# Low parts of the streamed weight blocks: a negated rounding on ScalarE and an accumulating GpSimd DMA instead of a VectorE subtraction

## The chip, the cores and the metric

The program runs on one NeuronCore of a Trainium2 chip. The metric is the device time of one execution in microseconds (us), and the time before is the median of three executions. Engines are named as in the profile: PE is TensorE's matmul stream and PEld its weight loads, DVE is VectorE, ACT is ScalarE, POOL is GpSimd, SP is SyncE, which in this kernel issues every DMA.

## The reference, cut to what matters

One inference step of a two-layer encoder trunk over 656 tokens (16 meta tokens, 512 prompt tokens, 8 streams of 16 new tokens), all in float32. Per layer:

```
h    = rmsnorm(x, g_mix);  proj = h @ w_in                 # 1024 -> 3072 columns
qa, ka, va, glu, zf, ic, qc, gc = split(proj)
oa   = differential attention (4 heads, relative-position bias, chunk mask)
ob   = swish(layernorm(causal depthwise conv of GLU, width 31))
oc   = gated linear recurrence (4 heads, 64 x 64 state)
x    = x + concat(oa, ob, oc) @ w_out                      # 1024 -> 1024
h2   = rmsnorm(x, g_ffn);  gate, val = split(h2 @ w_up)    # 1024 -> 2 x 2816
x    = x + (gelu(conv3(gate)) * val) @ w_down              # 2816 -> 1024
```

The outputs are the normalised x and the new keys, values and states. The weight products are wanted with nearly float32 accuracy, which is why both operands of each are split into two parts.

## The kernel before, in words

**Layout and products.** Channels lie on the 128 partitions, the 656 token columns on the free axis, in two halves of 328. Weights come from HBM in blocks of 128 x 128; a *block column* is the column of such blocks that makes 128 output channels. `w_load` (L327 to L331) gets a block column with one DMA of SP into a tile `raw`, of which the pool has NR = 3 buffers. `w_split` (L336 to L351) turns it into units of up to four row blocks (three where there are six): ACT rounds `raw` to the type fp32r in L347, which gives `whi`, and DVE makes `wlo = raw - whi` in L348. Both have NW = 4 buffers. The activations are split in the same way (`split`, L314). `mm3` (L356 to L361) then issues three matmuls for each row block, in the order hi times `whi`, lo times `whi`, hi times `wlo`, and adds them up in PSUM. So PE first needs a unit's `wlo` at its third matmul.

**Units kept apart.** With `own=True` the two parts go to buffers of the large pool `slots` (`ghi`, `glo`); this is used where a unit must be ready long ahead, at the start of a layer's projection and of the feed-forward, and in the last stage of the program. The feed-forward's gates and values are made by Strassen's method in `combos` (L938): POOL adds and subtracts weight halves (`wcb`, L944), and ACT and DVE split the results at L950 and L951, in the same four `whi` and `wlo` buffers.

**Stages of a layer.**

- Input projection: 24 block columns of eight row blocks, the first three together as a group. Between them stand the generators of attention, convolution and recurrence (`advance`), so DVE, ACT and POOL have much other work here.
- Output projection, first part (`d_oa`): 8 block columns of six row blocks, then the second part (`d_ob`): 8 of two row blocks, each followed by the residual add (`add_x`, L404), a square (L395, summed on POOL at L400) and the split of x (L322, L323).
- Feed-forward: pairs of gate and value block columns (G, V in the string FFN), and between them the down projection in parts (D0, D1, D2 of six row blocks, 8 block columns each; D3 of four). `add_x` adds each product to x. D3 of layer 0 also squares and splits x for the next layer; D3 of the last layer is the program's last stage, with `own` units.

**What sets the order.** The program is written in one order; a scheduler then sorts the instructions of each engine's queue by its own estimate, allots pool buffers and sets the waits. Every engine works its queue strictly in order. A conversion at L347 waits for its `raw` to land and for PE to have finished with the unit that held its `whi` buffer; with four buffers that is the unit four places before. A load waits until the last reader of its `raw` buffer is done. At the kernel's very start `start["on"]` keeps a few instructions in the written order (`seq`).

The lines the prediction speaks of:

```python
            seq(A.copy(hi[:, :n], raw[:, a:a + n]))
            seq(V.tensor_tensor(out=lo[:, :n], in0=raw[:, a:a + n], in1=hi[:, :n].bitcast(F32), op=ALU.subtract))
```

```python
        for j, (ww, r) in enumerate(((whi, hi), (whi, lo), (wlo, hi))):
            PE.matmul(ps[:, :b - a], lhsT=ww[:, n], rhs=r[:, a:b], start=first and j == 0, stop=last and j == 2)
```

Of the kernel before, what the change touches and what calls it, by code (L numbers as in the profile page):

```python
# [9 lines left out]
F32 = mybir.dt.float32  # L10
# [3 lines left out]
ALU = mybir.AluOpType  # L14
# [7 lines left out]
T = 656  # L22
# [22 lines left out]
# columns in two parts: all; behind 12 meta tokens; behind all meta tokens  # L45
# [9 lines left out]
# columns of the packed small operands  # L55
# [36 lines left out]
def pack(x):  # L92
    """layouts only: channels to rows, weights in blocks of 128 x 128"""
# [6 lines left out]
    small = dict(cst)  # L100
# [34 lines left out]
def unpack(r):  # L135
    """layouts only: back to the shapes of the reference"""
# [18 lines left out]
def trunk_kernel(ctx: ExitStack, tc: tile.TileContext, i: dict, o: dict, depth: int = 2):  # L155
# [51 lines left out]
    # gains that go with norm_r, which gives -2 / rms  # L207
# [21 lines left out]
    def setup():  # L229
# [35 lines left out]
        # relative-position bias times 8 (scores are scaled by 1/8 together with it)  # L265
# [25 lines left out]
    def norm_r(ones, srcs, nm, cc=CA):  # L291
        """-2 (ones^T-sum of srcs + eps) ** -0.5 on all partitions: table value and one Newton step."""
# [16 lines left out]
    def seq(ins):  # L309
        """in the order of the program at the kernel's start, where all inputs are on their way"""  # L310
        if start["on"]:
            tc.keep_in_program_order(ins)
            start[ins.ins.engine] = ins.ins
# [22 lines left out]
    def w_split(raw, kt, a=0, own=False):  # L336
        """hi and lo parts of row blocks a..kt: [(hi, lo, place in unit)] by k"""
        half = 4 if kt in (4, 8) else 3
        units = []
        while a < kt:  # L340
# [7 lines left out]
            seq(V.tensor_tensor(out=lo[:, :n], in0=raw[:, a:a + n], in1=hi[:, :n].bitcast(F32), op=ALU.subtract))  # L348
# [20 lines left out]
    def gemm(units, ks, rhs, nm, cc=CA, P=PD):  # L369
        """two psum[128, columns] = w^T rhs, float32 operands as hi + lo parts"""  # L370
        return [gemm1(units, ks, rhs, f"{c}_{nm}", cc[c], P) for c in range(2)]

    def gemm_group(unit_lists, ks, rhs, nm, cc=CA):
        """three products side by side, in the order in which the row blocks of rhs come"""
# [16 lines left out]
    def sq_add(m, ab=(0, T)):  # L391
        """accumulate x_m ** 2"""
# [20 lines left out]
    def tok_major(src, nm):  # L413
        """[128 tokens, 4, 128] of tokens 0..511, then [:, 512:640] samples; second tile: tokens 512..527."""
# [14 lines left out]
    def attention(l, h, got, mix):  # L429
# [32 lines left out]
        # prompt queries, tiles of 128 behind the meta tokens  # L462
# [59 lines left out]
        # running streams; the meta queries as a ninth stream without past keys  # L522
# [116 lines left out]
    def conv(l, t, got, accs):  # L639
# [11 lines left out]
        # last 30 inputs of each stream  # L651
# [629 lines left out]
```

## Time and profile before

| | |
|---|---|
| three executions, median (lowest, highest) | 1781.49 us (1781.0, 1783.29) |
| profiled execution, first to last instruction (its span) | 1784.5 us |
| mean granted TensorE clock | 0.968 |
| PE busy | 1650.5 us, 92% |
| PEld busy | 1550.3 us, 87% |
| DVE busy | 1327.3 us, 74% |
| ACT busy | 820.6 us, 46% |
| POOL busy | 596.2 us, 33% |
| bytes moved by DMA | 151.19 MB, 85 GB/s on average |

For the profiled execution the page gives its span, 1784.5 us, and no other time of its own. That is 3.0 us (0.17%) above the median of the three executions and 1.2 us above the slowest of them. A busy share is a mean over stages with different limits, so the sections below go by stage. Matmuls are pipelined: one record lasts 0.31 us, but in a dense stretch one starts every 0.15 us.

### The profile page before, as it was taken

The page shows a single profiled execution, that of the slowest core. Times are in us where ns is not written, and L with a number is a line of the kernel's source. Part 1 is how long each engine was busy: PE and PEld are TensorE (multiplying, and loading weights), DVE is VectorE, ACT ScalarE, POOL GpSimd, SP SyncE. Part 2 cuts the span into 40 slices and gives each one's busy share as a digit, 9 for nine tenths or more (in the row PEclk, how much of TensorE's full clock was granted, in tenths as well). Part 3 has the DMA queues.
Part 4 walks back from the last instruction along what each step waited for, and adds up shares of the span by engine and source line. Part 5 has one row for each costly group of instructions (what it writes and reads, how often), then busy time and mean ns, then how long its engine had stood idle before and what let it go on. Part 6 is the DMA issues. An engine that isn't in the chain of part 4 may idle for free.

```text
span 1784.5 us, 28714 instructions
## 1 busy us (share of the span) xinstructions
PE 1650.5 (92%) x10760; PEld 1550.3 (87%) x10760; DVE 1327.3 (74%) x2492; ACT 820.6 (46%) x1605; POOL 596.2 (33%) x620
## 2 busy tenths in 40 slices
PE   7769899999899999999999989899998999999897
PEld 6759687898889989988999978788988998999896
DVE  6159998759995884788556799866898668568855
ACT  5156364745442342444336545566535334343524
POOL 2012222004661551764021132300266256156503
PEclk9989999999999999999999999999999999999999
DMA  5223211234124222222332211213412422222132
GB/s 183 43 77 92 74 63 55 73 123 141 38 66 148 71 72 71 71 83 73 123 117 71 78 64 66 73 53 113 174 36 69 135 72 69 86 71 83 58 90 71
DMA packets 62270, 151.19 MB, mean 85 GB/s; under 512 B 11284, under 2 KB 16916, under 8 KB 62132
## 3 DMA queue, kind: packets, MB, share of 16 engines
q1 hardware_dynamic: 62132, 149.36, 25.8%
q8 instruction: 85, 1.39, 0.3%
q14 instruction: 53, 0.43, 0.1%
HBM read 129.80 MB, written 19.54 MB: 84 GB/s over the span
## 4 chain that ended last, share of the span: by engine, by line
PE 56%; DVE 23%; POOL 6%; DMA 5%; issue 5%; ACT 3%; DVEq 0%; SPq 0%; POOLq 0%; ACTq 0%
PE d_dn L361 16%; PE d_i L361 11%; PE d_v L361 6%; PE d_oa L361 5%; PE d_g L361 4%; DMA raw<-in_w_in 3%; POOL wcb L944 3%; DVE wlo L951 3%; DMA raw<-in_w_up 2%; PE e_i L361 2%; POOL gv L1210 2%; DVE fh L1025 2%; DVE ga L1047 2%; DVE cva L676 2%; PE sc L478 1%
## 5 line engine op out<-in xcount | busy, mean ns | idle before, releaser
L347 ACT CAST whi<-raw 128x384 fp32r<-128x384 f32 (+2 forms) x243 | 132.1, 547 | 330.7 <-PE d_dn L361 107.7
L361 PE MATMUL d_v<-fh,whi 128*128 128x328 f32 (+1 forms) x1120 | 261.2, 321 | 11.7 <-DVE gp L1173 6.2
L361 PE MATMUL d_g<-fh,whi 128*128 128x328 f32 (+1 forms) x1008 | 235.4, 321 | 11.9 <-ACT us_g L984 10.9
L361 PE MATMUL d_i<-hi_h,whi 128*128 128x328 f32 x672 | 219.1, 326 | 22.8 <-ACT whi L347 21.9
L348 DVE TENSOR_TENSOR wlo<-raw,whi 128x384 fp32r<-128x384 f32 (+2 forms) x243 | 155.3, 644 | 91.9 <-ACT whi L347 83.9
L361 PE MATMUL d_i<-lo_h,whi 128*128 128x328 f32 x672 | 215.5, 321 | 0.0
L361 PE MATMUL d_i<-hi_h,wlo 128*128 128x328 f32 x672 | 214.6, 319 | 0.0
L361 PEld LDWEIGHTS d_v<-fh,whi 128*128 128x128 f32 x1120 | 195.3, 195 | 15.8 <-ACT ga L1049 7.4
L361 PE MATMUL d_dn<-lo_g,whi 128*128 128x328 f32 (+1 forms) x640 | 199.1, 311 | 0.0
L361 PE MATMUL d_dn<-hi_g,whi 128*128 128x328 f32 (+1 forms) x640 | 198.8, 311 | 0.0
L361 PE MATMUL d_dn<-hi_g,wlo 128*128 128x328 f32 (+1 forms) x640 | 198.6, 310 | 0.0
L361 PE MATMUL d_v<-fh,wlo 128*128 128x328 f32 (+1 forms) x560 | 180.3, 322 | 14.6 <-DVE wlo L951 14.6
L361 PEld LDWEIGHTS d_g<-fh,whi 128*128 128x128 f32 x1008 | 176.8, 196 | 14.6 <-ACT us_g L984 12.4
L944 POOL TENSOR_TENSOR wcb<-raw 128x512 f32<-128x512 f32 x76 | 110.7, 1457 | 213.9 <-DMA raw<-in_w_up 193.8
L361 PE MATMUL d_g<-fh,wlo 128*128 128x328 f32 (+1 forms) x504 | 161.5, 320 | 5.5 <-DVE wlo L951 5.5
L950 ACT CAST whi<-wcb 128x512 fp32r<-128x512 f32 x152 | 94.0, 619 | 150.8 <-POOL wcb L944 68.0
L361 PEld LDWEIGHTS d_i<-hi_h,whi 128*128 128x128 f32 x672 | 128.0, 190 | 32.3 <-ACT whi L347 22.2
L951 DVE TENSOR_TENSOR wlo<-wcb,whi 128x512 fp32r<-128x512 f32 x152 | 130.1, 867 | 25.7 <-ACT whi L950 24.7
L951 DVE TENSOR_TENSOR wlo<-raw,whi 128x512 fp32r<-128x512 f32 x114 | 126.2, 1107 | 16.1 <-ACT whi L950 15.8
L361 PEld LDWEIGHTS d_i<-lo_h,whi 128*128 128x128 f32 x672 | 127.6, 190 | 4.6 <-issue 2.4
L361 PEld LDWEIGHTS d_i<-hi_h,wlo 128*128 128x128 f32 x672 | 127.8, 190 | 3.5 <-issue 1.8
L361 PEld LDWEIGHTS d_v<-fh,wlo 128*128 128x128 f32 x560 | 109.2, 195 | 18.4 <-DVE wlo L951 18.3
(387 smaller groups left out, 4085.0 us busy)
## 6 DMA issues: line engine op xcount, KB each, us to landing
raw<-in_w_up SPq DMA_DIRECT2D x88, 512.0 KB, 3.5
raw<-in_w_in SPq DMA_DIRECT2D x45, 512.0 KB, 3.7
raw<-in_w_down SPq DMA_DIRECT2D x48, 384.0 KB, 3.1
x_scr<-x SPq DMA_DIRECT2D x24, 328.0 KB, 2.3
x<-x_scr SPq DMA_DIRECT2D x24, 328.0 KB, 5.3
raw<-in_w_out SPq DMA_DIRECT2D x16, 384.0 KB, 3.1
x<-in_x SPq DMA_DIRECT2D x16, 328.0 KB, 5.7
cache_k<-in_cache_k SPq DMA_DIRECT2D x16, 256.0 KB, 4.1
```

What stands on the lines that cost most here:

```text
L347: seq(A.copy(hi[:, :n], raw[:, a:a + n]))
L348: seq(V.tensor_tensor(out=lo[:, :n], in0=raw[:, a:a + n], in1=hi[:, :n].bitcast(F32), op=ALU.subtract))
L361: PE.matmul(ps[:, :b - a], lhsT=ww[:, n], rhs=r[:, a:b], start=first and j == 0, stop=last and j == 2)
L478: PE.matmul(ps[:, o0:o0 + w], lhsT=q[64 * c:64 * c + 64, q0:q0 + 128], rhs=k[64 * c:64 * c + 64, n * w:(n + 1) * w], start=True, stop=True)
L676: V.scalar_tensor_tensor(out=ap_, in0=up, scalar=wj, in1=ap_, op0=ALU.mult, op1=ALU.add)
L944: G.tensor_tensor(out=t, in0=x, in1=y, op=op)
L950: A.copy(hi, x)
L951: V.tensor_tensor(out=lo, in0=x, in1=hi.bitcast(F32), op=ALU.subtract)
L1025: V.tensor_tensor(out=lo, in0=x, in1=hi.bitcast(F32), op=ALU.subtract)
L1047: V.scalar_tensor_tensor(out=a[:, a0:n], in0=g[:, 1 + a0:1 + n], scalar=fw(1), in1=a[:, a0:n], op0=ALU.mult, op1=ALU.add)
L1210: G.tensor_tensor(out=v[:, a0:TP], in0=v[:, a0:TP], in1=a[:, a0:TP], op=ALU.mult)
```

## The change

In `w_split`, for units that are neither `own` nor part of the group at the kernel's start, DVE's subtraction is replaced by two steps. ACT writes `-1 * raw`, rounded to fp32r, into `lo`; this is the negated `hi`, since rounding is symmetric. Then POOL issues a DMA from `raw` to `lo` that adds to what is there, so that `lo` holds `raw - hi`.

```diff
             seq(A.copy(hi[:, :n], raw[:, a:a + n]))
-            seq(V.tensor_tensor(out=lo[:, :n], in0=raw[:, a:a + n], in1=hi[:, :n].bitcast(F32), op=ALU.subtract))
+            if own or start["on"]:
+                seq(V.tensor_tensor(out=lo[:, :n], in0=raw[:, a:a + n], in1=hi[:, :n].bitcast(F32), op=ALU.subtract))
+            else:
+
+                A.mul(lo[:, :n], raw[:, a:a + n], -1.0)
+                nc.gpsimd.dma_start(out=lo[:, :n].bitcast(F32), in_=raw[:, a:a + n], accum_op=ALU.add)
             units += [(hi, lo, m) for m in range(n)]
```

The rest of the diff drops comments. Lines behind this place are numbered five higher in the changed kernel (the matmuls of L361 are at L366); its new steps are at L352 (ACT) and L353 (the DMA of POOL).

240 of DVE's 243 subtractions into `wlo` at L348 go: 96 of 128x512, 128 of 128x384 and 16 of 128x256. ACT gains 240 instructions of these shapes, POOL 240 DMAs. The 37 subtractions into `glo`, and the 266 of `combos` at L951, stay.

DVE's queue in the input projection of layer 0, between two evictions of products (`e013`, `e014`; `cva` is the convolution, `hst` and `otok` belong to the recurrence). Before:

```order
L386 TENSOR_TENSOR e013_1643<-d_1_i013_1618,r_h0_211 128x328
...
L859 TENSOR_REDUCE otok_1681<-hst000_1684 128x64
L859 TENSOR_REDUCE otok_1681<-hst001_1691 128x64
L348 TENSOR_TENSOR wlo_1756<-raw_1753,whi_1755 128x512
L348 TENSOR_TENSOR wlo_1760<-raw_1753,whi_1759 128x512
L676 SCALAR_TENSOR_TENSOR cva00_1209<-u00_1071,cst_82,cva00_1209 128x528
L386 TENSOR_TENSOR e014_1750<-d_0_i014_1700,r_h0_211 128x328
```

After:

```order
L391 TENSOR_TENSOR e013_1665<-d_1_i013_1640,r_h0_211 128x328
...
L864 TENSOR_REDUCE otok_1705<-hst000_1708 128x64
L862 TENSOR_TENSOR hst001_1715<-hsi001_1713,cst_82 128x512
L682 SCALAR_TENSOR_TENSOR cva01_1360<-us01_1235,cst_82,cva01_1360 128x128
L864 TENSOR_REDUCE otok_1705<-hst001_1715 128x64
L681 SCALAR_TENSOR_TENSOR cva01_1360<-u01_1234,cst_82,cva01_1360 128x528
L682 SCALAR_TENSOR_TENSOR cva01_1360<-us01_1235,cst_82,cva01_1360 128x128
L391 TENSOR_TENSOR e014_1774<-d_0_i014_1724,r_h0_211 128x328
```

The two subtractions are gone, and steps of the convolution have moved between the recurrence's.

ACT's queue at the start of the down projection D0 of layer 0 (`ga` are gates). Before:

```order
L347 CAST whi_5511<-raw_5509 128x384
L347 CAST whi_5515<-raw_5509 128x384
L1046 ACTIVATE ga06_5443<-gp06_5292,cst_82 128x672
L1046 ACTIVATE ga07_5450<-gp07_5295,cst_82 128x672
L347 CAST whi_5563<-raw_5561 128x384
L1049 ACTIVATE ga06_5443<-ga06_5443 128x672
L1049 ACTIVATE ga07_5450<-ga07_5450 128x672
L347 CAST whi_5567<-raw_5561 128x384
```

After:

```order
L347 CAST whi_5581<-raw_5579 128x384
L352 ACTIVATE wlo_5582<-raw_5579 128x384
L347 CAST whi_5586<-raw_5579 128x384
L352 ACTIVATE wlo_5587<-raw_5579 128x384
L1051 ACTIVATE ga06_5511<-gp06_5360,cst_82 128x672
L1051 ACTIVATE ga07_5518<-gp07_5363,cst_82 128x672
L347 CAST whi_5635<-raw_5633 128x384
L1054 ACTIVATE ga06_5511<-ga06_5511 128x672
L352 ACTIVATE wlo_5636<-raw_5633 128x384
L1054 ACTIVATE ga07_5518<-ga07_5518 128x672
L347 CAST whi_5640<-raw_5633 128x384
L352 ACTIVATE wlo_5641<-raw_5633 128x384
```

Each rounding is followed by its negated copy, once with a gate's activation between them.

POOL's queue at the same place (`wcb` is the last combination of the gates before it, `gout` the gates' saved columns). Before:

```order
L944 TENSOR_TENSOR wcb_5420<-raw_5300,wcb_5342 128x512
L1041 COPY gout0_4450<-gp07_5295 128x2
L1042 COPY gout0_4450<-gp07_5295 128x16
L1041 COPY gout0_4450<-gp06_5292 128x2
L1042 COPY gout0_4450<-gp06_5292 128x16
```

After:

```order
L949 TENSOR_TENSOR wcb_5488<-raw_5368,wcb_5410 128x512
L353 DMA wlo_5528<-raw_5525 128x384
L353 DMA wlo_5533<-raw_5525 128x384
L353 DMA wlo_5582<-raw_5579 128x384
L1046 COPY gout0_4516<-gp07_5363 128x2
L1047 COPY gout0_4516<-gp07_5363 128x16
L1046 COPY gout0_4516<-gp06_5360 128x2
L1047 COPY gout0_4516<-gp06_5360 128x16
L353 DMA wlo_5587<-raw_5579 128x384
```

The first three accumulates of the stage stand behind the last combination and ahead of the `gout` copies; each waits for its copy on ACT.

## Rows read from the trace of the kernel before

**Rows 1.** The page, span and busy time by engine

```profile
span 1784.5 us, 28714 instructions
...
PE 1650.5 (92%) x10760; PEld 1550.3 (87%) x10760; DVE 1327.3 (74%) x2492; ACT 820.6 (46%) x1605; POOL 596.2 (33%) x620
```

**Rows 2.** Busy time by stretch: start:end and length, then by engine (instructions)

```profile
core 0: us, PE busy (x) PEld busy (x) DVE busy (x) ACT busy (x) POOL busy (x), PEclk, DMA share, GB/s
150.00:200.00 50.00, 44.45 (x283) 40.56 (x282) 49.77 (x89) 25.94 (x53) 16.56 (x12) 0.95 0.24 81
...
540.00:583.00 43.00, 43.00 (x290) 43.00 (x289) 20.11 (x37) 11.39 (x21) 5.22 (x9) 1.00 0.34 116
1000.00:1050.00 50.00, 50.00 (x332) 47.12 (x331) 46.14 (x90) 25.96 (x57) 14.80 (x13) 0.97 0.20 66
```

**Rows 3.** Chain of waits, shares by line: 102:350, 350:435, 540:583, 960:1214, 1214:1300

```profile
by line: PE d_i L361 30.3%; DVE cva L676 6.0%; PE sc L478 4.1%; DVE cva L677 4.0%; issue 3.7%; PE hl L768 3.5%; PE po L514 3.0%; DVE wlo L348 3.0%; DVE e L386 1.9%; PE aTp L502 1.6%; PE ho L904 1.3%; DVE p L492 1.3%; PE po L517 1.3%; PE np_
...
by line: PE d_oa L361 52.8%; DVE lo_h L323 6.1%; issue 5.8%; PE d_ob L361 5.6%; DVE x L404 4.5%; DVE wlo L348 4.0%; PE po L514 2.9%; PE sc L478 2.6%; PE aTp L502 1.7%; PE po L517 1.5%; PE np_on L299 1.3%; ACT r_h L300 1.1%; ACT rt_h L301 1.
...
by line: PE d_dn L361 100.3%; PE d_v L361 0.4%
...
by line: PE d_i L361 34.1%; DVE cva L676 5.8%; issue 3.7%; DVE wlo L348 3.5%; PE sc L478 3.1%; PE po L514 3.0%; DVE e L386 3.0%; DVE cva L677 2.8%; PE hl L768 2.5%; DVE e L432 1.9%; PE np_qn L299 1.8%; DVE p L480 1.6%; POOL p L491 1.3%; PE 
...
by line: PE d_oa L361 51.3%; issue 6.0%; DVE lo_h L323 5.9%; PE d_ob L361 5.4%; DVE x L404 4.3%; DVE wlo L348 3.9%; PE po L514 2.8%; PE sc L478 2.5%; DVE x L1003 1.9%; PE aTp L502 1.7%; PE po L517 1.4%; PE np_on L299 1.3%; ACT r_h L300 1.1%
```

**Rows 4.** Groups by line and shape: busy us, mean ns, idle before, releasers

```profile
L348 DVE TENSOR_TENSOR wlo<-raw,whi 128x384 fp32r<-128x384 f32 x128 | 72.4, 570 | 46.3 <-ACT whi L347 38.7 <-ACT sot L589 4.9 <-DMA raw<-in_w_up 2.6
L348 DVE TENSOR_TENSOR wlo<-raw,whi 128x512 fp32r<-128x512 f32 x99 | 72.3, 738 | 41.8 <-ACT whi L347 41.4
L348 DVE TENSOR_TENSOR wlo<-raw,whi 128x256 fp32r<-128x256 f32 x16 | 10.6, 660 | 3.8 <-ACT whi L347 3.8
L347 ACT CAST whi<-raw 128x384 fp32r<-128x384 f32 x128 | 65.4, 512 | 185.9 <-PE d_dn L361 98.6 <-issue 31.5 <-PE d_g L361 22.0
L347 ACT CAST whi<-raw 128x512 fp32r<-128x512 f32 x99 | 60.3, 616 | 128.7 <-PE d_i L361 70.5 <-DMA raw<-in_w_in 31.0 <-issue 14.1
L347 ACT CAST whi<-raw 128x256 fp32r<-128x256 f32 x16 | 6.5, 403 | 16.1 <-PE d_oa L361 7.5 <-PE d_ob L361 5.0 <-DMA raw<-in_w_out 2.8
```

**Rows 5.** A DMA issue on SP's queue (timeline), POOL's costliest group (page)

```profile
537.52 0.33 SPq L330 DMA_DIRECT2D raw<-in_w_down  x1
...
L944 POOL TENSOR_TENSOR wcb<-raw 128x512 f32<-128x512 f32 x76 | 110.7, 1457 | 213.9 <-DMA raw<-in_w_up 193.8
```

**Rows 6.** The page, DMA issues: count, KB each, median us to landing

```profile
raw<-in_w_down SPq DMA_DIRECT2D x48, 384.0 KB, 3.1
...
raw<-in_w_in SPq DMA_DIRECT2D x6, 256.0 KB, 6.1
out_y<-y SPq DMA_DIRECT2D x8, 192.0 KB, 2.0
```

**Rows 7.** Timeline inside D0, layer 0: a unit's rounding, its first wlo matmul

```profile
549.23 0.51 ACT L347 CAST whi<-raw 128x384 fp32r<-128x384 f32 x1 [3.14 <-issue]
...
556.16 0.31 PE L361 MATMUL d_dn<-hi_g,wlo 128*128 128x328 f32 x1
```

**Rows 8.** Timeline at the start of D0, layer 1: the same for unit two

```profile
1398.27 0.51 ACT L347 CAST whi<-raw 128x384 fp32r<-128x384 f32 x1 [1.27 <-PE d_g L361]
...
1403.42 0.31 PE L361 MATMUL d_dn<-hi_g,wlo 128*128 128x320 f32 x1
```

**Rows 9.** Timeline in the output projection's second part, layer 0: the same

```profile
406.99 0.41 ACT L347 CAST whi<-raw 128x256 fp32r<-128x256 f32 x1 [1.44 <-DMA raw<-in_w_out]
...
411.92 0.31 PE L361 MATMUL d_ob<-hi_mx,wlo 128*128 128x328 f32 x1
```

**Rows 10.** Timeline at the late load of layer 0's projection: the same

```profile
101.06 1.14 ACT L347 CAST whi<-raw 128x512 fp32r<-128x512 f32 x2 [27.14 <-DMA raw<-in_w_in]
...
102.46 0.64 PE L361 MATMUL d_i<-hi_h,wlo 128*128 128x328 f32 x1
```

**Rows 11.** Timeline early in layer 0's projection: the same

```profile
49.07 0.62 ACT L347 CAST whi<-raw 128x512 fp32r<-128x512 f32 x1 [5.03 <-PE d_i L361]
...
58.33 0.31 PE L361 MATMUL d_i<-hi_h,wlo 128*128 128x328 f32 x1
```

## The prediction, made before the changed kernel ran

> **What bounds the kernel now.** I read the page's busy times first: PE works 1650.5 us of a span of 1784.5, 92%, DVE 74%, ACT 46%, POOL 33% [rows 1]. Work moved from DVE to ACT and POOL therefore pays only where PE waits for DVE. The table by stretch says where that can be [rows 2]. Inside the input projections DVE is full or nearly so: 49.77 of 50 us at 150 to 200 and 46.14 at 1000 to 1050, while ACT has half its time left and POOL two thirds. But PE works 44.45 us of the first stretch and all 50.00 of the second, so even there only the first has room. Inside D0 PE works 43.00 of 43 us and DVE 20.11: no engine but PE sets anything.
>
> The chain of waits, taken by stage, prices that [rows 3]. The subtraction L348 holds 3.0% of 102:350 (248 us), 4.0% of 350:435 (85), 3.5% of 960:1214 (254) and 3.9% of 1214:1300 (86). These are 7.4, 3.4, 8.9 and 3.4 us, together 23.1. In D0's stretch PE's own matmuls hold 100.3%, the subtraction nothing. So 23 us is the most that its removal can return.
>
> **What leaves DVE and comes to ACT and POOL.** DVE's wlo groups hold 155.3 us in 243 instructions, at 570, 738 and 660 ns by shape [rows 4]; 240 go, some 153 us. ACT's new step reads and writes the same tiles as its rounding, so I price it by that: 128 x 0.512 + 96 x 0.616 + 16 x 0.403 = 65.5 + 59.1 + 6.4 = 131 us. ACT would rise from 821 to about 950 us. POOL gains 240 DMA issues. No row has POOL issuing one; SP's issue takes 0.33 us, POOL's common 128x512 step 1457 ns [rows 5]. Between these it gains 79 to 360 us; at about 0.9, nearer to neither, some 216, to about 810 us, under half of the span.
>
> **The unknown, L.** Call L the time from the end of ACT's negated copy to a usable `wlo`: semaphore to POOL, POOL's issue, the transfer that reads `raw` and `lo` and writes `lo`, the semaphore to PE. It replaces one subtraction of 0.57 to 0.74 us. No DMA of before moves between two on-chip tiles or adds. The nearest rows are the output's store of 192 KB, the size of a 128x384 part, at 2.0 us from issue to landing, the down weights' load of 384 KB at 3.1, and a load of 256 KB in the crowded start at 6.1 [rows 6]. The bounds are 2.0 and 6.1. I take 4.0, twice the store, since an addition must read what it adds to as well as the source; the store is the nearest row in size, in its on-chip source and in a calm stretch.
>
> **Where L lies beside other work.** PE needs `wlo` only at a unit's third matmul, so the question is how long after the start of its rounding this matmul comes. The new path is rounding, negated copy, L.
> - *Steady down projection.* A rounding at 549.23 serves a matmul at 556.16: 6.93 us [rows 7]. The new path takes 2 x 0.51 + 4.0 = 5.0. Cost 0; the cover is PE's work on earlier units in four buffers. It is gone at L = 5.9.
> - *Second unit of each of the six starts of D0 to D2.* 1403.42 - 1398.27 = 5.15 us [rows 8]; 5.02 fits with 0.1 to spare. Cost 0, gone at L = 4.1.
> - *Second part of the output projection.* 411.92 - 406.99 = 4.93 us is among its tightest [rows 9]; 2 x 0.40 + 4.0 = 4.8. Cost 0, gone at the same L.
> - *The block column whose load is late, input projection of layer 0.* ACT has waited for the load, and the first matmul with `wlo` follows the rounding's start by 102.46 - 101.06 = 1.40 us [rows 10]: nothing covers it. 2 x 0.62 + 4.0 - 1.40 = **+3.8 us**.
> - *Other units of the input projections:* 58.33 - 49.07 = 9.26 us is early in the stage and the shortest but those of the late column [rows 11]; 2 x 0.62 + 4.0 = 5.2. Cost 0.
> - *`raw` buffers*, three, are held about 4.5 us longer, until the addition has read them. D's 290 matmuls in 43 us [rows 2] are 0.148 us each; three block columns of 6 x 3 x 2 matmuls take 16.0 us. In that time a buffer must pass a landing, half a column's wait for its second unit, two roundings with their copies and an addition, 3.1 + 2.7 + 2.0 + 4.0 = 11.8 us: cost 0. SP's queue holds loads that wait for `raw` anyway; what is late next, if this cover goes, is the next block's rounding.
>
> **What queues behind.** POOL works in order, so an accumulate that waits for ACT's copy holds what is behind: at D0's start the `gout` copies, which nobody awaits there; in the projections attention's products and the convolution's sums. On ACT a rounding now stands behind another's copy, and gates behind both. ACT and POOL have half their time free in the projections, so I charge **+2 us** over both layers, about a tenth of the 23.1 that the chain has there.
>
> **What DVE gives back.** Half of the chain's share: where the chain runs through the subtraction, DVE's next step is often due anyway (a convolution step or eviction stands next in the queue), and 1000 to 1050 shows PE already without a gap [rows 2], 150 to 200 with 5.5 us of them. 16.3/2 + 6.8/2 = 8.1 + 3.4 = **-11.5 us**.
>
> **The sum** is -11.5 + 2 + 3.8 = -5.7 us. It is made against the profiled execution, 1784.5 us of span, 3.0 above the median of the runs, 1781.49. The page gives no time around the span, so I carry the difference to the median: about 1776 us. A measurement of this kernel can tell about 0.2%, 3.6 us, from no change.
>
> **Rivals.**
>
> *A, the forecast:* L up to 4.1, half the chain's share returns. **1776**, 1772 to 1779 as L and the share vary a little. For it: the slack in the steady stretches. Against: no row shows L. Chance 0.40.
>
> *B, late at the starts only:* L between 4.1 and 5.9. At L = 5.0 the late column costs 4.8, six starts 6 x 0.87 = 5.2, and the second output part about four stalls (two a layer) of 0.9, 3.6; with -11.5 + 2 the sum is +4, **1786**. For it: a margin of 0.1 us at the starts is thin, and there POOL's first accumulates stand behind the last weight combination, a step of 1457 ns [rows 5]. Against: 3.1 us sufficed for a load of twice the bytes. Chance 0.20.
> The Trainium skill, "DMA: Bandwidth & Descriptors", section "Specifications", puts the first byte at about 1 us for DMAs of GpSimd and 0.6 for those of SyncE. No row of before tests that; an estimate of L by it is 0.4 above mine, 4.4, and the sum about -2.
>
> *C, slower, the down projection waits for the accumulate.* It decides at L = 5.9. A rounding there waits for the unit four before, so an excess e = 1.02 + L - 6.93 returns once in four units, that is two block columns; 48 block columns of six rows (six stages of eight) pay it 24 times. At L = 6.1: 24 x 0.19 = 4.6, starts 6 x 1.97 = 11.8, late column 5.9, output part 4 x 2.0 = 8; less the 9.5 that is won, +21, **1802**. At L = 7 it is +52 in the same way, **1834**. For it: the row of 6.1 us in a crowded stretch; D already streams 116 GB/s [rows 2], and the additions move more than as many bytes again beside it; POOL's issues are priced by nothing. Against: the same stretch lands 384 KB in 3.1 us [rows 6], and DVE has half its time free. Chance 0.20.
> The Trainium skill, "SBUF — State Buffer", section "SBUF: two separate sides", has GpSimd's writing of a DMA's descriptors shut out while DVE runs an instruction that takes the port both share; the section after it gives 620 ns that became 3100. Whether DVE's steps here do that no row of before shows; an estimate of L by it is 4.0 + 2.5 = 6.5, and the sum by C about +35. In C's chance it is included.
>
> *D, ACT or POOL takes back what DVE gives.* ACT's 131 us fall where the chain also passes its roundings, and POOL's issues delay attention: a gain of 0 to 4, and with the late column **1783**. Against: half of ACT is idle there. Chance 0.12.
>
> *E, the whole share returns:* -23.1 + 2 + 3.8 = -17, **1764**. Against: PE's 50.00 of 50. Chance 0.08.
>
> That the change doesn't do what it says is excluded by the order of the instructions: 240 subtractions are gone, though 37 into `glo` and 266 of `combos` stay.
>
> **Numbers.** Forecast 1776, the likeliest case's. The range must reach down to E, 1764, and up through B into C, to 1805, C at L a little over 6.1; beyond lies about a tenth at the top, less below. A's own range is 1772 to 1779. Faster by over 0.2% (below 1778): E 0.08, most of A 0.33, a little of D, 0.02: 0.43. Slower (above 1785): C 0.20, most of B 0.12, D 0.02: 0.34. Within: 0.23.
>
> **What would show each step.** In the changed profile: three subtractions into `wlo` left and DVE down by some 153 us; 240 new ACT steps at 0.4 to 0.6 us; the page's DMA issues with `wlo<-raw` and its landing, from which L follows; PE's idle time before D's matmuls ended by the DMA into `wlo`, nearly none in A, 6 times in B, every other block column in C. Around 101 us PE's stall grows by 4. In the projections the chain loses L348; if its share reappears on other DVE steps, half was too much, and if on ACT's new line or POOL, D holds. L above 4.1 makes the forecast wrong, well above 4.4 its sign; POOL's issue far above 1.5 us would do so by itself.

## The result and the profile after

| | before | changed |
|---|---|---|
| median of four runs (lowest, highest), us | 1782.11 (1781.0, 1783.29) | 1830.03 (1827.9, 1832.89) |
| ratio, 95% interval | | 1.0268 (1.025 to 1.0286) |
| span of the profiled execution, us | 1784.5 | 1827.6 |

The changed kernel is 47.9 us slower, where 1776 was forecast. The spans differ by less, 43.1 us: a span is about 1.8 us shorter than the time of its execution (1827.6 and 1829.4 for the changed kernel), so the 1784.5 of the kernel before belongs to an execution of some 1786 us, 4 above the median. The engines' share is much as the prediction had it. The page of the changed kernel, against [rows 1], with the groups of the new steps and the landing times (groups: instructions, busy us, mean ns, idle before and its releasers; DMA issues: count, KB each, median us to landing):

```profile
PE 1660.4 (91%) x10760; PEld 1556.2 (85%) x10760; DVE 1191.5 (65%) x2252; ACT 923.4 (51%) x1843; POOL 800.2 (44%) x860
...
L353 POOL DMA_DIRECT2D wlo<-raw x240 | 208.9, 882 | 489.5 <-ACT wlo L352 427.0
...
L352 ACT ACTIVATE wlo<-raw 128x384 fp32r<-128x384 f32 (+2 forms) x240 | 133.1, 555 | 0.0
...
wlo<-raw POOLq DMA_DIRECT2D x96, 256.0 KB, 3.8
wlo<-raw POOLq DMA_DIRECT2D x128, 192.0 KB, 4.0
wlo<-raw POOLq DMA_DIRECT2D x16, 128.0 KB, 3.2
```

DVE's busy time fell by 136 us and the span still grew by 43.1. ACT's new steps hold 133.1 us, POOL's issues 882 ns each, 208.9 us, and an addition lands 3.2 to 4.0 us after its issue (medians of the three sizes). No engine is fuller than PE, so the 43 us are PE's: 33 of them are idle time, and 10 are its busy time, which grew from 1650.5 to 1660.4 us for the same 10760 matmuls. Where they lie is read from the timeline: the table takes the last matmul of each stage (of the stage's own products, in the rows of L366 and L361), and gives by how many us the stage got longer than in the kernel before, measured from the end of the stage ahead of it.

| stage | layer 0 | layer 1 | both |
|---|---|---|---|
| input projection | +5.9 | -3.9 | +2.0 |
| output projection, first part | +0.7 | +1.0 | +1.7 |
| output projection, second part | +14.9 | +11.2 | +26.1 |
| feed-forward's gates and values, in sum | -1.2 | -5.0 | -6.2 |
| D0 | +4.5 | +3.6 | +8.1 |
| D1 | -0.1 | +0.2 | +0.1 |
| D2, and D3 of layer 0 | +8.1 | +2.7 | +10.8 |

How much of this is the spread of single traces is told by six kernels of the experiments that have no addition in the projections (additions in the second output part alone, its shadow, the packed loads without additions, and the three of the down parts). Read in the same way, they give -1.4 to -0.4 us for layer 0's projection and -3.1 to +2.7 for layer 1's, and -1.8 to +1.5 and -6.1 to -0.9 for the gates and values. So the -3.9 and -5.0 of layer 1 are no gain that this table shows. The output projection and the down parts repeat within 0.3 us where they are unchanged.

In D0 of layer 0, past its start, nothing is lost: the chain there is PE's own matmuls, as in [rows 3], though the DMA's share has gone from 0.34 [rows 2] to 0.72. Table by stretch and chain by line of the changed kernel in that stretch:

```profile
566.00:608.00 42.00, 42.00 (x276) 42.00 (x275) 10.23 (x19) 14.33 (x29) 14.91 (x15) 0.98 0.72 169
```

```profile
by line: PE d_dn L366 100.9%
```

Three other places have to be read. **First, layer 0's projection around the write of the bias table.** The timeline at its start (start us, us, engine, line, operation), then the chain of waits in 60:114 (start us, us, what), of the changed kernel:

```profile
42.57 0.83 SPq L277 DMA_DIRECT2D bias_scr<-fs  x1
48.87 0.85 POOL L353 DMA_DIRECT2D wlo<-raw  x1 [9.71 <-ACT wlo L352]
50.68 0.85 POOL L353 DMA_DIRECT2D wlo<-raw  x1 [0.95 <-ACT wlo L352]
```

```profile
57.93 41.06 DMA wlo<-raw
99.00 0.04 issue
99.04 14.53 PE d_i L366 x81
```

The addition issued at 57.93, while the table is being written, lands 41 us later. In the kernel before only the late load stood in that write [rows 10]; the units already loaded were finished by DVE without any DMA. Now each of them needs one. Six additions went out in 40:105 (count, KB each, median us to landing):

```profile
wlo<-raw POOLq DMA_DIRECT2D x6, 256.0 KB, 29.1
```

PE's waits in 40:110, changed kernel, then the kernel before (what, us in total, times, longest):

```profile
PE d_i L366 <- DMA wlo<-raw: 28.6, 4, 17.6
```

```profile
PE d_i L361 <- ACT whi L347: 21.9, 1, 21.9
```

**Second, the second part of the output projection.** SP's waits there in the changed kernel (414:448), then the same in the kernel before (404:426):

```profile
SPq L330 <- DMA wlo<-raw: 18.8, 6, 4.9
SPq L412 <- DVE x L409: 10.6, 6, 2.6
```

```profile
SPq L407 <- DVE x L404: 8.0, 5, 3.8
SPq L330 <- DVE wlo L348: 4.6, 4, 2.4
```

SP waited 4.6 us for DVE to release raw buffers and now waits 18.8 for additions to do it. The chain in the same stretch of the changed kernel runs through additions, loads and POOL's sums of squares:

```profile
409.99 5.69 DMA wlo<-raw
...
415.74 2.24 DMA raw<-in_w_out
...
418.05 1.04 issue
...
419.10 2.67 DMA wlo<-raw
...
429.64 1.55 POOL sq L405
431.19 3.25 DMA wlo<-raw
```

The waits are not all that this stage pays. Its granted clock fell. Table by stretch of the stage in the kernel before, then in the changed one, with a part of it (the third figure from the end is PEclk), and PE's timeline at the start of that part:

```profile
408.17:425.78 17.61, 14.94 (x97) 14.33 (x97) 16.44 (x26) 10.67 (x18) 7.96 (x5) 1.00 0.64 216
```

```profile
414.84:447.34 32.50, 24.37 (x114) 22.27 (x114) 18.34 (x28) 16.24 (x31) 15.50 (x13) 0.81 0.65 177
421.80:427.90 6.10, 6.10 (x22) 6.10 (x23) 2.31 (x4) 2.12 (x5) 2.19 (x3) 0.50 0.73 197
```

```profile
421.80 0.64 PE L366 MATMUL d_ob<-hi_mx,wlo 128*128 128x328 f32 x1 [2.70 <-DMA wlo<-raw]
```

PE had waited 2.70 us for an addition, and in the 6.10 us that follow the granted clock is 0.50, the lower of its two levels (1.2 instead of 2.4 GHz): a matmul starts every 0.27 us, against 0.15 in a dense stretch of before. In this stage 40 matmuls of layer 0 and 28 of layer 1 start at that pace. I estimate from this that some 5 and 3 of its 14.9 and 11.2 us are the clock, and the rest mostly waits.

**Third, the start of D0**, layer 0, in the chain of the changed kernel: the first unit's addition takes 7.38 us, in a stretch where the loads of `in_w_down` and `x_scr` go out too, and PE waits 2.5 us for it.

```profile
556.49 7.38 DMA wlo<-raw
```

### The profile page after: what moved, and what is told of

Read it like the earlier page. It is cut to its first block, busy times and chain, and to the rows that moved or that the text cites. A ratio compares the mean times of both kernels' runs of the same rounds, so it can differ in the third digit from the quotient of the medians.

```text
span 1827.6 us, 29407 instructions
## 1 busy us (share of the span) xinstructions
PE 1660.4 (91%) x10760; PEld 1556.2 (85%) x10760; DVE 1191.5 (65%) x2252; ACT 923.4 (51%) x1843; POOL 800.2 (44%) x860
## 4 chain that ended last, share of the span: by engine, by line
PE 46%; DVE 19%; DMA 12%; issue 10%; POOL 8%; ACT 4%; SPq 0%; POOLq 0%; DVEq 0%; ACTq 0%
PE d_i L366 11%; PE d_dn L366 9%; PE d_v L366 7%; DMA wlo<-raw 7%; PE d_g L366 4%; DMA raw<-in_w_up 3%; POOL wcb L949 3%; DVE wlo L956 2%; DVE fh L1030 2%; DVE cva L681 2%; POOL gv L1215 2%; POOL wlo L353 2%; DVE ga L1052 2%; PE d_oa L366 2%; DVE cva L682 1%
## 5 line engine op out<-in xcount | busy, mean ns | idle before, releaser
L353 POOL DMA_DIRECT2D wlo<-raw x240 | 208.9, 882 | 489.5 <-ACT wlo L352 427.0
L366 PE MATMUL d_v<-fh,whi 128*128 128x328 f32 (+1 forms) x1120 | 261.0, 321 | 18.4 <-DVE gv L978 11.3
L366 PE MATMUL d_i<-hi_h,wlo 128*128 128x328 f32 x672 | 216.9, 323 | 29.6 <-DMA wlo<-raw 29.6
L366 PE MATMUL d_g<-fh,whi 128*128 128x328 f32 (+1 forms) x1008 | 230.5, 317 | 9.5 <-ACT us_g L989 7.9
L366 PE MATMUL d_i<-hi_h,whi 128*128 128x328 f32 x672 | 219.9, 327 | 0.9 <-DVE e L391 0.9
L366 PEld LDWEIGHTS d_v<-fh,whi 128*128 128x128 f32 x1120 | 195.2, 195 | 23.9 <-ACT ga L1054 14.1
L366 PE MATMUL d_i<-lo_h,whi 128*128 128x328 f32 x672 | 215.5, 321 | 0.0
L366 PE MATMUL d_dn<-hi_g,wlo 128*128 128x328 f32 (+1 forms) x640 | 201.5, 315 | 10.9 <-DMA wlo<-raw 10.8
L366 PE MATMUL d_dn<-hi_g,whi 128*128 128x328 f32 (+1 forms) x640 | 200.0, 313 | 1.8 <-DVE x L409 1.8
L366 PE MATMUL d_dn<-lo_g,whi 128*128 128x328 f32 (+1 forms) x640 | 200.1, 313 | 0.0
L366 PE MATMUL d_v<-fh,wlo 128*128 128x328 f32 (+1 forms) x560 | 180.8, 323 | 14.1 <-DVE wlo L956 14.1
L366 PEld LDWEIGHTS d_g<-fh,whi 128*128 128x128 f32 x1008 | 172.8, 192 | 12.0 <-ACT us_g L989 9.3
L366 PE MATMUL d_g<-fh,wlo 128*128 128x328 f32 (+1 forms) x504 | 159.0, 315 | 4.7 <-DVE wlo L956 4.7
L366 PEld LDWEIGHTS d_i<-hi_h,wlo 128*128 128x128 f32 x672 | 129.2, 192 | 33.7 <-DMA wlo<-raw 31.3
L409 DVE TENSOR_TENSOR x<-d_dn,x 128x328 f32<-128x328 f32 (+1 forms) x112 | 54.3, 493 | 156.7 <-PE d_dn L366 149.6
L366 PEld LDWEIGHTS d_i<-hi_h,whi 128*128 128x128 f32 x672 | 129.4, 193 | 10.1 <-issue 3.6
L366 PEld LDWEIGHTS d_dn<-hi_g,wlo 128*128 128x128 f32 x640 | 120.9, 189 | 14.7 <-DMA wlo<-raw 14.5
L352 ACT ACTIVATE wlo<-raw 128x384 fp32r<-128x384 f32 (+2 forms) x240 | 133.1, 555 | 0.0
```

The source lines that it names most:

```text
L352: A.mul(lo[:, :n], raw[:, a:a + n], -1.0)
L353: nc.gpsimd.dma_start(out=lo[:, :n].bitcast(F32), in_=raw[:, a:a + n], accum_op=ALU.add)
L409: V.tensor_tensor(out=xs[m][:, a:b], in0=ps[c][:, :b - a], in1=xs[m][:, a:b], op=ALU.add)
```

## The experiments

The runs of the kernel before beside them had medians of 1781.9 to 1783.8 us. Two theories stood at the outset: the loss sits where an addition stands in POOL's queue behind steps that wait for PE, and where another transfer holds DMAs up (Q); or it goes with the traffic (B). `dve["on"]` and its like are flags that a stage sets around its calls.

**Without additions in the second output part.**

```diff
-            if own or start["on"]:
+            if own or start["on"] or kt == 2:
```

> The changed kernel, but the 16 units of the output projection's second part (128x256) are made by the VectorE subtraction again; the other 224 are as changed. Theory Q (the loss sits where an accumulate stands in POOL's queue behind the sums of squares of the previous block columns, and where DMA is closed): the stage got 26 us longer over both layers (14.9 and 11.2 by the trace), so about 1804 us, 1800 to 1808. Rival B (the extra DMA traffic slows every transfer, the loss goes with the number of additions): 16 of 240 additions, 3 of 48 us, about 1827.

1825.99 us, ratio 1.0239 (1.0222 to 1.0256). Neither theory: the second part is still 7.2 and 5.3 us too long, with no addition of its own. Whatever causes that comes from the stage ahead.

**The sums of squares off POOL.**

```diff
-            (V if m == 7 else G).tensor_tensor(out=t[:, a:b], in0=t[:, a:b], in1=sq[:, a:b], op=ALU.add)
+            V.tensor_tensor(out=t[:, a:b], in0=t[:, a:b], in1=sq[:, a:b], op=ALU.add)
```

> All 240 additions as changed, but the sums of the squares of x stand on VectorE, not on POOL. Theory Q: POOL's queue has no step left that waits for the previous product, so most of the 34 us of the second output part (26) and of layer 0's last down part (8) returns, about 1800 us, 1796 to 1810. Rival L (the transfer's own time, or ACT's copy behind other steps of ACT, makes those stages late): little returns, 1820 or more.

1834.87 us, 1.0284 (1.0266 to 1.0301): nothing returned; the stage is 14.0 and 13.6 us too long. POOL's order is not what sets it, and Q falls there. What the chain shows now (414:450) is the loop that replaced it:

```profile
413.36 6.51 DMA wlo<-raw
...
419.94 2.22 DMA raw<-in_w_out
...
422.22 1.03 issue
...
423.27 2.66 DMA wlo<-raw
...
425.98 4.58 DMA raw<-in_w_out
```

Addition, load, addition, load: a raw buffer is reloaded only when its addition has read it. A new theory follows, R: the three raw buffers are the limit where block columns are short.

**DVE for the units around the table's write** (block columns 3 to 8 of layer 0).

```diff
-            if own or start["on"]:
+            if own or start["on"] or dve["on"]:
...
+                dve["on"] = l == 0 and n + 1 <= 8
                 nxt = weights(w[col[n + 1]], 0, 8)
```

> The changed kernel, but the units of the block columns 3 to 8 of layer 0's projection, those that are split before and during the write of the bias table, are made by VectorE's subtraction. Theory Q: an addition issued at 48.87 us landed at 99, with the table's write under way; without that the 13 us that layer 0's projection had lost by 101 us return, about 1817 us, 1813 to 1821. Rival: PE is held there by the late load anyway, as in the kernel before, and nothing returns, 1828 to 1832.

1825.18 us, 1.0238 (1.0208 to 1.0269). The median returned 5 us, but these runs spread over 12 (1821.35 to 1833.81), so the stage says more: the projection of layer 0 ended 5.9 us late in the changed kernel and ends 4.4 us early here, 10.3 us. Other kernels bear it out: the six with additions around the table, the changed one among them, read +5.9 to +10.1 us for this stage, and the two without, -4.4 here and -3.9 in the next experiment. PE's wait in 40:110 is again the late load's, as before:

```profile
PE d_i L368 <- ACT whi L349: 22.0, 1, 22.0
```

**Additions in the input projections alone**, and not around the table: the same flag, and one more that is set at the projections' start and cleared at their end.

```diff
-            if own or start["on"]:
+            if own or start["on"] or dve["on"] or kt != 8 or not proj["on"]:
```

> Additions only in the input projections, and in layer 0 only from block column 9 on; all other units by VectorE's subtraction. Theory Q: what is left is DVE's relief in the projections, which the trace of the changed kernel puts at 6 us a layer; 1782 - 12, about 1770 us, 1766 to 1776. Rival B (traffic): under a third of the loss stays with under a third of the additions, 1785 to 1797. Rival D (ACT's copies and POOL's issues take back what DVE gives): 1778 to 1784.

1781.14 us over ten runs against 1783.71, 0.9984 (0.9974 to 0.9994). It is faster than both kernels, than the one before by 2.6 us, under 0.2% but with an interval clear of 1. By stages the projections are 3.9 and 3.6 us shorter. DVE is as full as before in 150:200:

```profile
150.00:200.00 50.00, 44.33 (x286) 40.55 (x284) 49.77 (x86) 29.90 (x59) 26.78 (x23) 0.96 0.55 132
```

So it is not 12. The 7.5 us by stages hold some of the spread told above: the six kernels without additions there average -0.7 in layer 0 and -1.3 in layer 1. Against these, the two kernels that spare the table (-4.2 on average in layer 0) and the eight with additions throughout layer 1's projection (-4.6) leave about 3.4 us a layer. Whole runs gain 2.6; where the difference goes is not shown.

**Raw buffers held, nothing late.**

```diff
+            if not (own or start["on"]):
+                nc.gpsimd.dma_start(out=hold[held[0] % 16][:, :n], in_=raw[:, a:a + n])
```

> VectorE makes every low part as before and ACT writes no negated copy, but POOL issues for each of the 240 units a DMA that copies the raw block to HBM scratch: nothing waits for that copy except the buffer's next load. So it adds the hold of the three raw buffers, POOL's issues and about the traffic, and takes away the lateness of the low part itself. Theory R (the raw buffers, held until the addition has read them, are reloaded late, and the stages of short block columns run at that loop's pace): second output part and layer 0's last down part stay slow, about 1782 + 26 + 8 = 1816, 1808 to 1826. Theory L (PE waits for each low part itself): 1780 to 1788.

1798.56 us, 1.0092 (1.0064 to 1.012), a miss for both: the second output part is only 1.6 and 0.8 us longer; the projections are 6.7 and 4.4 longer, where the spread told above goes up to -0.4 and +2.7. The copy is a weaker hold than the addition: it does not wait for ACT, and it lands in 2.6 us. POOL's groups and the DMA issues of this kernel:

```profile
L353 POOL DMA_DIRECT2D hold<-raw x240 | 131.7, 551 | 583.1 <-DMA raw<-in_w_in 258.5 <-DMA raw<-in_w_out 167.6 <-DMA raw<-in_w_down 140.0
```

```profile
hold<-raw POOLq DMA_DIRECT2D x96, 256.0 KB, 2.6
hold<-raw POOLq DMA_DIRECT2D x128, 192.0 KB, 2.5
```

**Packed loads**: in the second output part four short block columns share a raw buffer, in layer 0's D3 two; and the same in the kernel before, as a control.

```diff
+            for j in range(per):
+                nc.sync.dma_start(out=pk["raw"][:, j * kt:(j + 1) * kt], in_=w[m + j, :, k0 * 128:(k0 + kt) * 128].rearrange("p (k n) -> p k n", n=128))
+        a = m % per * kt
+        return w_split(pk["raw"], a + kt, a)
...
-                nxt = weights(wo[m + 1], 6, 2)
+                nxt = packed(wo, m + 1, 6, 2, 4)
```

> All 240 additions as changed, but in the second output part four block columns share one raw buffer, and in layer 0's last down part two: each buffer is reloaded a quarter or half as often. Theory R: those two stages get most of their 34 us back, about 1803, 1797 to 1812. Theory L: each addition lands as late as before, 1822 to 1834.

> The control of the packed loads: the kernel before with the same packing. By theory R its buffers are not the limit, so nothing changes by more than 4 us: 1778 to 1786; if packing itself shortens or lengthens these stages, that is to be taken off the gain of the packed change.

1822.97 us, 1.0225 (1.0197 to 1.0252), and the control 1.0002 (0.999 to 1.0014). The second part's loss fell from 14.9 and 11.2 to 7.0 and 6.4, half. Of the 8.1 us of layer 0's D2 and D3, 6.8 stayed, but all of it in D2: D3, whose loads are packed, is as long as before. So R is part of it, and what stays is as large as in the first experiment.

**Additions in the second output part alone** (`kt != 2` on DVE).

> Additions only in the 16 units of the output projection's second part; all others by VectorE. Without them 14 of that stage's 26 us came back and 12 stayed. If the two halves are separate (the rest comes from the first part's buffers being held), this costs 14, about 1796, 1791 to 1800; if the loop of loads in the stage itself makes nearly all, 1802 to 1810; theory L alone (a late low part at two places a layer) 1784 to 1788.

1798.85 us, 1.0082 (1.0058 to 1.0107): 8.5 and 10.9 us in that stage. Alone, with the stage ahead undisturbed, it costs 15 us by whole runs, 19.4 by the stage.

**The shadow**: DVE makes the low part that PE uses; ACT and POOL do the change's work beside it, on a spare tile.

```diff
+            if kt == 2 and not own:
+                j = junk.tile([128, 128], F32R, tag="junk", name="junk")
+                A.mul(j, raw[:, 0], -1.0)
+                nc.gpsimd.dma_start(out=j.bitcast(F32), in_=raw[:, 0], accum_op=ALU.add)
```

> The kernel before, and in the 16 units of the second output part a shadow of the change: VectorE makes the low part that PE uses, and beside it ACT writes the negated first block of the unit to a spare tile (four buffers) and POOL's accumulating DMA adds the raw block to it; no one waits for the sum but the raw buffer's next load. It adds the hold of the buffers and POOL's queue, and leaves out that PE waits for the sum. Additions in this stage alone cost 15 to 19 us. If they cost it through the buffers (theory R): 1793 to 1800. If through the lateness at PE (theory L): 1782 to 1787.

1791.01 us, 1.0045 (1.0029 to 1.0062); the stage is 5.9 and 6.2 us longer, against 8.5 and 10.9. So 12.1 of the stage's own 19.4 us (8 of 15 by whole runs) come without PE waiting for any sum: from held buffers and from the queues of ACT and POOL, which the shadow does not separate. The other 7.3 us go with PE's wait, or with the shadow's smaller addition, half of a unit; the granted clock, 0.85 and 0.89 there and 0.93 and 1.00 with the shadow, is part of them.

**No additions in either output part.**

```diff
-            if own or start["on"]:
+            if own or start["on"] or oa["on"]:
```

> The changed kernel, but neither part of the output projection has additions. With additions in the first part alone the second part still lost 7.2 and 5.3 us. Theory H (the last units of the first part hold their raw buffers, so the loads of the feed-forward's first blocks and of the second part start late): those 12 us return against the 1826 measured without additions in the second part, about 1813, 1808 to 1817. Rival (something else in layers and traffic makes the stage late): 1822 to 1830.

1813.81 us, 1.0165 (1.014 to 1.019): the second part is 0.0 and 0.1 us longer, 12 us less than with the first part's additions. Those 12 us are a handover. The first part's last units hold the raw buffers, so the loads of the feed-forward's first weights and of the second part start late, and ACT's queue then waits for these loads. A step of ACT's timeline near the end of the first part, in the kernel before, then in the run without additions in the second part:

```profile
402.21 1.14 ACT L347 CAST ghi<-raw 128x512 fp32r<-128x512 f32 x2 [0.49 <-DMA raw<-in_w_up]
```

```profile
415.74 1.14 ACT L347 CAST ghi<-raw 128x512 fp32r<-128x512 f32 x2 [4.16 <-DMA raw<-in_w_up]
```

**Packed, and the first output part by DVE.**

> All additions as changed except in the first part of the output projection, and the packed loads (four short block columns share one raw buffer). The second part has its 16 additions still. Theories R and H together: the remaining 7.0 and 6.4 us return against the 1823 of the packed kernel, about 1810, 1805 to 1815, and the stage ends within 2 us of the kernel before. If lateness at PE is what remains (L): 1819 to 1827.

1811.73 us, 1.0169 (1.0137 to 1.02). The second part keeps its 16 additions and is -0.6 and +0.2 us longer, and its granted clock is 1.00 again (layer 0):

```profile
418.17:435.39 17.22, 15.18 (x100) 14.63 (x99) 14.30 (x21) 13.01 (x24) 13.47 (x12) 1.00 0.92 251
```

Held buffers and handover together, with the fall of the clock behind them, are the whole 26 us of that stage: with both loosened, an addition's own lateness costs nothing there.

**The subtraction on POOL**, in the input projections, instead of ACT's copy and the DMA.

```diff
+            eng = G if proj["on"] and not own and not start["on"] else V
-            seq(V.tensor_tensor(out=lo[:, :n], in0=raw[:, a:a + n], in1=hi[:, :n].bitcast(F32), op=ALU.subtract))
+            seq(eng.tensor_tensor(out=lo[:, :n], in0=raw[:, a:a + n], in1=hi[:, :n].bitcast(F32), op=ALU.subtract))
```

> The kernel before, with the subtraction of the input projections' units (block columns from the fourth on, both layers) on POOL in place of VectorE: no negated copy, no DMA. POOL's step of the same shape and two operands takes 1457 ns, VectorE's 738, and POOL is idle two thirds there. If DVE's relief is what the projection-only kernel won, this wins at least as much, 1782 - 4 to 1782 - 12, 1770 to 1778; if POOL's longer step and its queue cost more than they free, 1782 or more.

1810.23 us, 1.0143 (1.0119 to 1.0167), a miss. PE waits only 0.4 us for POOL; DVE's steps are what gets longer. Groups of DVE in the kernel before, then in this one:

```profile
L676 DVE SCALAR_TENSOR_TENSOR cva<-u,cst,cva 128x528 f32<-128x528 f32 x88 | 74.0, 841 | 0.0
L677 DVE SCALAR_TENSOR_TENSOR cva<-us,cst,cva 128x128 f32<-128x128 f32 x88 | 37.7, 429 | 0.0
```

```profile
L679 DVE SCALAR_TENSOR_TENSOR cva<-u,cst,cva 128x528 f32<-128x528 f32 x88 | 80.1, 910 | 0.0
L680 DVE SCALAR_TENSOR_TENSOR cva<-us,cst,cva 128x128 f32<-128x128 f32 x88 | 49.5, 563 | 0.0
```

The same convolution steps take 910 and 563 ns instead of 841 and 429, and DVE's busy time is 1323.5 us against 1327.3 although 84 subtractions have left it. These means mix several cases. Where no step of POOL overlaps them, they take 757 and 340 ns in the kernel before and 755 and 339 here. The 13 and 17 that overlap one of POOL's subtractions take 1588 and 1104 on average. And where only POOL's issue of an addition is under way, they take 757 and 340 in the changed kernel (22 and 14 of them): an issue doesn't slow them.

**The down parts.** Additions in layer 0's D3 alone (`kt != 4` on DVE), in D0 to D2 alone, and the shadow in D3.

> Additions only in the 8 units of the last down part of layer 0 (four row blocks); all others by VectorE. In the changed kernel this part lost 8.1 us and kept 6.9 of them with packed loads. If the part's own additions cost that: 1782 + 7 = 1789, 1787 to 1792. If it was the traffic of the rest or of the stage before: 1781 to 1784.

> Additions only in D0, D1 and D2 of both layers, 96 units, 40% of all. By the trace of the changed kernel the starts of D0 cost 4.4 and 2.7 us, single late units about 3 more, and D1 nothing: 1782 + 8 to 10 = 1791, 1787 to 1795. If a cost goes with the number of additions or the traffic (theory B): 40% of 48, 1801.

> The kernel before with the shadow (negated copy of the first block and the addition to a spare tile, the low part by VectorE) in the 8 units of layer 0's last down part. Through the hold of the raw buffers and POOL's queue behind the sums of squares: 1786 to 1791. Through lateness at PE: 1781 to 1784.

D3 alone: 1784.22 us, 1.0011 (1.0002 to 1.0021), and its stage is 0.0 us longer, so the stage doesn't suffer from its own additions alone. D0 to D2 alone: 1800.11 us, 1.0097 (1.0082 to 1.0112), more than I expected: D0 costs 5.0 and 4.9 us at its starts, D1 0.0 and 0.6, and D2 4.6 and 6.0, where PE waits 2.1 us (layer 0) and 3.0 (layer 1) in one piece for a unit of the last block column. That is the handover again. The waits are smaller than the stages' loss; the granted clock is 0.96 in each of these four stages and was 1.00. The time is what theory B had put it at, 1801, but the places are not: D1, with a third of these additions, pays almost nothing. In the changed kernel the 8.1 us are 3.6 in D2 and 4.5 in D3. The second share appears only where both have additions, and not always: it is nothing without additions in the output projection, where D2 loses 6.0, and nothing with packed loads, but 3.6 with packed loads and DVE in the first output part. No run takes that apart. The chain near D2's end in layer 0 of the run of D0 to D2 alone (840:925), SP's waits in 865:895 and a step of ACT's timeline:

```profile
875.73 4.57 issue
880.31 6.55 DMA wlo<-raw
886.91 35.72 PE d_dn L368 x226
```

```profile
SPq L330 <- DMA wlo<-raw: 10.0, 3, 4.3
SPq L330 <- DMA raw<-in_w_in: 7.2, 2, 3.9
```

```profile
878.04 1.14 ACT L349 CAST ghi<-raw 128x512 fp32r<-128x512 f32 x2 [3.46 <-DMA raw<-in_w_in]
```

SP's loads of the next layer's first weights wait for additions; on ACT the roundings of those weights stand ahead of D2's last block column, which therefore starts late and lands late. The shadow in D3: 1787.07 us, 1.003 (1.0018 to 1.0042). Its stage is 0.5 us longer, and 3.9 us come between it and the next layer's first product, which the additions themselves (1.5 there) do not show; where these come from stays open.

## Why the prediction was wrong, by its own steps

**Right: the engines' prices.** ACT's steps were put at 131 us and hold 133.1; a POOL issue at about 0.9 us and holds 0.882 (the upper bound of POOL's range, 240 steps of 1457 ns, is 350 us and not 360; nothing hangs on it). The steady down projection costs nothing, as its slack of 6.93 us [rows 7] said: D1 is 0.1 us longer in sum.

**Too small: L.** It was put at 4.0, and the forecast held up to 4.1. Pairing ACT's 240 copies in order with POOL's 240 additions, the issue follows 0.3 us after the copy in the median and about 1 us or more in a tenth, the landing 3.9 us after the issue, and L is 4.4 in the median; 141 are above 4.1 and 43 above 5.9. By the prediction's own sign the forecast was then wrong. But this is not what cost the 26 us: among the additions issued in the second output part the median L is 3.9 and 3.7.

**About right by stages: DVE's relief in the projections.** Half of the chain's share there was 8.1 us; with the spread of the traces taken off, the stages got about 7 shorter, and whole runs 2.6. In the output projection, 3.4 us more were booked; nothing of it came.

**Wrong: "raw buffers: cost 0".** This is the step that failed, and the largest part of the loss. I worked the loop out for D alone, where three block columns take PE 16 us. In the second output part a block column has a third of the matmuls, the kernel before took 17.8 us for eight (408.0 to 425.8), so three last 6.7 us, and load, rounding, copy and addition need 2.2 + 0.4 + 0.4 + 0.3 + 3.2 = 6.5 with the median landing of these additions, and landings go up to 5.7 in the chain above. That, and the buffers handed over late at the end of the first part, cost 26 us (the packed run with the first part on DVE gives all of it back), and D2, with the handover at its end, 4.6 and 6.0 in the run of D0 to D2 alone. The unit's own slack of 4.93 us [rows 9] that I held against L was the wrong quantity: it told when PE wants the sum, not when SP wants the buffer.

**Missing: the clock.** The sum priced each wait once. In the second output part the granted clock fell from 1.00 to 0.81 and 0.82 while PE kept waiting, by my estimate some 8 of the 26 us; the mean over the whole span fell from 0.968 to 0.962.

**Wrong: "late column +3.8".** I gave an addition under the table's write the same L as elsewhere, and let [rows 10] count one late unit. The row itself told of a DMA stuck there: ACT waited 27.14 us for the load. Six additions were issued in that time, and the projection of layer 0 was 10 us worse for it. That it is the table's write that holds them is argued from the time: no run takes the write away.

**Too small: the starts.** One L for all places hid the spread. At D0's starts, where loads collide with the first additions, one took 7.38 us; D0 cost 8.1 us in the changed kernel and 10.0 alone. Rival B had priced 5.2 for all six starts at L = 5.0. D1's two starts cost 0.1.

**The rivals.** The time is that of rival C at L = 7, but its mechanism did not take place: no steady stall, and L at 4.4 in the median. That its number fits is luck. What happened is nearest to B, with a condition B lacked. Theory B of the experiments (traffic) is against the records: past D0's start the DMA's share doubled and PE lost nothing, and 16 additions of 240 cost 15 us. The parts do not add exactly: D0 to D2 alone cost 18, the second output part alone 15, which leaves some 15 for the handover from the first output part and the table, less the relief.

The rule that I cited for C from the Trainium skill, "SBUF — State Buffer", section "SBUF: two separate sides", that DVE shuts out GpSimd's descriptors, speaks of DVE's instructions in a 2-port mode. Nothing like it shows in these traces: in 112:358, with DVE busy for 200 of 246 us, a POOL issue takes 883 ns and an addition of 256 KB lands in 3.4 us, and in 566:608, with DVE a quarter busy, 859 ns and, of 192 KB, 3.8. Whether any of these steps of DVE runs in that mode, no run shows. The other half of that rule, that a DVE step with two on-chip inputs and a GpSimd step that reads on-chip memory exclude each other at a shared port, fits the run with the subtraction on POOL, where DVE's small convolution step takes 340 ns by itself and 1104 beside a subtraction; that run does not show the port itself.

## What to carry to other kernels

When a step in the middle of a buffer's life is made longer, price it twice: against the consumer's slack, and against the buffer's loop (load, use, release) in the stage with the shortest period, and again where one stage hands its buffers to the next. A step that moves from an engine to a DMA inherits every long transfer that is under way, so look in the trace for the places where a load took many times its median. And where PE's waits come close together, look at the granted clock before and after: the matmuls behind the waits may get longer too. Additions by DMA were worth having only where the units were ready 9 us or more ahead, and there they gave 0.16%.

## What the runs showed of the hardware

An adding DMA between two on-chip tiles cost more here than a plain one of the same blocks to HBM: POOL spent 882 ns on its issue against 551, and it landed in 3.8 to 4.0 us against 2.5 to 2.6 (256 and 192 KB). Whether the addition or the destination makes the difference, no run shows. Additions issued while the table's write of 1312 KB was under way landed up to 41 us later; the late load of before [rows 10] stood in the same write. A DVE step of two on-chip inputs that takes 340 ns took 1104 on average beside POOL's elementwise subtraction, so that moving 84 subtractions off DVE left its busy time nearly unchanged; POOL's issue of a DMA did not lengthen it. And behind waits of PE the granted clock stood at 0.50 for some us, with a matmul every 0.27 us instead of 0.15.
